# Gates as 1 + tanh instead of sigmoid, in a decoder layer on one Trainium2 core

## The chip, the cores and the metric

The kernel runs on one core of a Trainium2 chip. Its engines run side by side, each through an instruction list of its own, in order: PE multiplies matrices, DVE and ACT do elementwise work, POOL a little more of it, and SP issues the DMA transfers. An engine stops at an instruction until the semaphores that it waits for have been raised by other engines or by a landed transfer. The metric is the device time of one execution in microseconds (us).

## What is computed

One decoder layer on 512 tokens of width 1024, all in float32, then a final norm. Its two attention branches have 8 heads each: one looks back over a window of 128, with sinks, the other attends to blocks of 256. What matters here:

```python
cs = jax.nn.silu(c)
mod = cs @ ada_w[l] + ada_b[l]
shift1, scale1, gate1, shift2, scale2, gate2 = jnp.split(mod, N_MOD, axis=-1)
h = modulate(rmsnorm(x, norm1_g[l]), shift1, scale1)
proj = h @ w_in[l]
qa, ka, va, qb, kb, vb, ga, gb = jnp.split(proj, offsets, axis=-1)
ya = swa_attention(...) @ w_branch_a[l]
yb = moba_attention(...) @ w_branch_b[l]
merged = jax.nn.sigmoid(ga) * ya + jax.nn.sigmoid(gb) * yb
x = x + gate1[:, None, :] * (merged @ w_out[l])
h2 = modulate(rmsnorm(x, norm2_g[l]), shift2, scale2)
y = jnp.square(jax.nn.relu(h2 @ w_mlp_in[l])) @ w_mlp_out[l]
x = x + gate2[:, None, :] * y
```

## The kernel before

Every float32 product is done as three matmuls of halves: `split` (L71, L72) lets ACT copy the upper half of a tile (names ending in h) and DVE subtract it to get the lower half (names ending in l), and `mm3` (L76 to L78) multiplies high by high, high by low and low by high. So each weight tile passes through DMA, ACT and DVE before PE can use it.

The program runs through these stages. Up to about 70 us: the conditioning vector (`cond`, on the tile `cs`), the first norm and modulation, and part of the input projection. From 70 to about 175 us: the eight windowed heads (tiles named with a: `sa`, `pa`, `ta`), with the q, k, v projections of the other branch (`pqk`) beside them. From about 150 us: the eight block-sparse heads (tiles with b: scores `sb`, probabilities `pb`, their transposes `tb`, split as `ptb`, and head outputs `ob`). Each head's softmax is an Exp activation on ACT at L438, one per 128 queries, after a maximum on DVE (L434, L437). Beside these heads, `run` advances a generator of dense work by the numbers in the table PACE. In this stage that work is `gated(0, keep)`: for each 128 of the 1024 output channels n it makes a gate (`pg` = h times a slice of w_in, weights `gw0n`, then the sigmoid into `sg` at L568) and, one step later, a slice of the branch's output projection (`py`, weights `bw0n`), and `keep` (L593) multiplies the two into `term[n]`. A second generator, `mod_second`, advanced beside it, makes the modulation of the second norm (`ac` at L149 and L151, `pm` at L158) from loads named `a`.

From about 263 to 345 us the heads are over and `gated(1, merge)` does the same for the second branch. `merge` (L672) multiplies, adds `term[n]`, splits the sum into `mhi` and `mlo`, and `first` multiplies the former sum with w_out into `wo`, with weights `ow` from the load `wor`. Beside it `mod_row` builds the row of gate1 (tile `ma` from loads `mw`, sums over partitions in `pr`, bias added at L193). After 345 us come the second norm and the MLP: matmuls into `ph` and `mo`, last into `ml`.

PE is bound to the written order in the early stage and near the second norm; elsewhere a scheduler sets the order of all engines when the program is built. Weight loads share three buffers (`raw`), and the DMA into one is issued on SP once the last reader of its former content, mostly a DVE instruction, is through. ACT evaluates functions from a table that holds one set at a time: where an activation needs a function that the set loaded does not hold, the build puts an ACT_TABLE_LOAD ahead of it, which shows in the profile as an instruction of that activation's line.

Of the kernel before, what the change touches and what calls it, by code (L numbers as in the profile page):

```python
# [10 lines left out]
F32 = mybir.dt.float32  # L11
F32R = mybir.dt.float32r
AF = mybir.ActivationFunctionType
ALU = mybir.AluOpType

P = 128
D = 1024
S = 512
KT = D // P
# [18 lines left out]
def decoder_layer(ctx: ExitStack, tc: tile.TileContext, x, c, ada_w, ada_b, norm1_g, norm2_g, w_in,  # L38
# [3 lines left out]
    V, A, G, SY = nc.vector, nc.scalar, nc.gpsimd, nc.sync  # L42

    pz = ctx.enter_context(tc.tile_pool(name="pz", bufs=1, side="right"))
# [5 lines left out]
    def bank(name):  # L50
        return ps.tile([P, 512], F32, tag="bank", name=name)

    def raw(name):
        return p0.tile([P, 2048], F32, tag="raw", name=name, bufs=3)
# [8 lines left out]
    def small(name):  # L63
        return ptile(p0, [P, 512], name, "s", 2)

    def scratch(name, dt=F32):
        return p0.tile([P, 512], dt, name=name, tag="t", bufs=3)

    def split(hi, lo, src):

        A.activation(hi, src, AF.Copy)  # L71
        V.tensor_tensor(lo, src, hi.bitcast(F32), op=ALU.subtract)  # L72

    def mm3(o, w, m, first=True, last=True, **kw):

        nc.tensor.matmul(o, w[0], m[0], start=first, stop=False, **kw)  # L76
        nc.tensor.matmul(o, w[0], m[1], start=False, stop=False, **kw)  # L77
        nc.tensor.matmul(o, w[1], m[0], start=False, stop=last, **kw)  # L78

    def at(pair, *idx):  # L80
        return tuple(t[idx] for t in pair)
# [4 lines left out]
    def chain(*gens):  # L86
        for g_ in gens:
            yield from g_
# [17 lines left out]
    def slot(n, name, dt=F32):  # L106

        return p0.tile([P, 512], dt, name=name, tag=f"slot{n}")
# [14 lines left out]

    cols = pz.tile([P, 64], F32, name="cols")
    cs = pz.tile([P, KT], F32, name="cs")
    bcol = cols[:, 0:48]

    def cond(crow):

        pst = bank("pst")  # L130
        nc.tensor.transpose(pst[:, :KT], crow, ident[:KT, :KT])
        A.activation(cs, pst[:, :KT], AF.Sigmoid)
        V.tensor_mul(cs, cs, pst[:, :KT])

    def rows(stack):
        pst = bank("pst2")
        nc.tensor.transpose(pst[:, :64], stack, ident[:64, :64])
        V.tensor_copy(cols, pst[:, :64])
# [25 lines left out]
        V.tensor_mul(ab[:, 1:2], ab[:, 1:2], cols[:, gain + f:gain + f + 1])  # L164
        V.tensor_add(ab[:, 0:1], pm[:, 0:1], bcol[:, b0:b0 + 1])

    def mod_row(v, dst, pool):

        for half in range(2):
            acc = pool.tile([P, 512], F32, name=f"ma{v}{half}", tag="macc", bufs=1)  # L170
            c0 = v * D + half * 512
            for kk in range(2):
                t = raw(f"mw{v}{half}{kk}").rearrange("p (k n) -> p k n", k=4)
                SY.dma_start(t, ada_w[0].rearrange("(k p) n -> p k n", p=P)[:, 4 * kk:4 * kk + 4, c0:c0 + 512])
                yield
                for k in range(4):
                    c1 = cs[:, 4 * kk + k:4 * kk + k + 1]
                    if kk + k == 0:
                        V.tensor_scalar(acc, t[:, k], c1, None, op0=ALU.mult)
                    else:  # L180
                        V.scalar_tensor_tensor(acc, t[:, k], c1, acc, op0=ALU.mult, op1=ALU.add)  # L181
                    if k % 2:
                        yield
            b = dst[half]
            SY.dma_start(b, ada_b[:, c0:c0 + 512].to_broadcast([P, 512]))
            ah, al = (p0.tile([P, 512], F32R, name=f"ma{v}{half}{i}", tag="t", bufs=3) for i in "hl")
            split(ah, al, acc)
            for _ in range(3):
                yield
            pr = bank(f"pr{v}{half}")  # L190
            nc.tensor.matmul(pr, ones_r, ah, start=True, stop=False)
            nc.tensor.matmul(pr, ones_r, al, start=False, stop=True)
            V.tensor_tensor(b, pr, b, op=ALU.add)  # L193
            yield

    ab2 = pz.tile([P, KT, 2], F32, name="ab2")
# [1 line left out]
    def mod_second():  # L198
        for f in range(KT):
            ad = ada_load(3, f, raw(f"a2{f}"))  # L200
            yield
            acc = pz.tile([P, 2, P], F32, name=f"ac2{f}", tag="acc2", bufs=1)
            yield from mod_cols(f, 3, 56, ad, acc, ab2[:, f])

    with ExitStack() as sa:
# [28 lines left out]
        with ExitStack() as ss:  # L234
# [134 lines left out]
            for f in range(KT):  # L369
                for i, _ in enumerate(project(f, 2 if f == 0 else 0, NT)):  # L370
# [4 lines left out]
                    if i == 2 and f + 2 in starts:  # L375
                        n = starts[f + 2]
# [147 lines left out]
        def cols_of(wr, half, name):  # L524
            w = wide(name)
            split(w[0], w[1], wr[:, :, half * P:(half + 1) * P])
            return w
# [23 lines left out]
        def gated(s, use):  # L551

            wr = br = sg = None
            wb = (w_branch_a, w_branch_b)[s]
            for n in range(KT + 1):
                m, before = n - 1, sg
                if n < KT:
                    if n % 2 == 0:
                        wr = raw(f"gr{s}{n}").rearrange("p (k n) -> p k n", k=KT)
                        SY.dma_start(wr, w0[:, :, (C_GA, C_GB)[s] + n * P:(C_GA, C_GB)[s] + (n + 2) * P])  # L560
                    w = cols_of(wr, n % 2, f"gw{s}{n}")
                    pg = bank(f"pg{s}{n}")
                    for k in range(KT):
                        mm3(pg, at(w, slice(None), k), at(hT, slice(None), k), first=k == 0, last=k == KT - 1)
                        if k == 3:
                            yield
                    sg = scratch(f"sg{s}{n}")
                    A.activation(sg, pg, AF.Sigmoid)  # L568
                    yield
                if m < 0:  # L570
                    continue
                if m % 2 == 0:
                    br = p0.tile([P, 4, 256], F32, name=f"br{s}{m}", tag="br")
                    cc = slice(m * P, (m + 2) * P)
                    if s == 0:
                        for g in range(2):
                            SY.dma_start(br[g * 64:(g + 1) * 64],
                                         wb[0, g * 256:(g + 1) * 256, cc].rearrange("(j d) n -> d j n", d=64))
                    else:
                        SY.dma_start(br, wb[0, :, cc].rearrange("(j p) n -> p j n", p=P))  # L580
                u = tuple(v.rearrange("p (j n) -> p j n", j=4) for v in small(f"bw{s}{m}"))
                split(u[0], u[1], br[:, :, (m % 2) * P:(m % 2 + 1) * P])
                py = bank(f"py{s}{m}")
                for k in range(4):
                    mm3(py, at(u, slice(None), k), at(attnT[s], slice(None), k), first=k == 0, last=k == 3)
                use(m, py, before)
                yield

        term = {}

        def keep(n, py, sg):
            term[n] = slot(n, f"term{n}")
            V.tensor_tensor(term[n], py, sg, op=ALU.mult)  # L593

        def run(heads, dense, per):

# [17 lines left out]
        def beside(gen, other, n):  # L614
            for _ in gen:
                advance(other, n)
                yield

        ms = mod_second()
        second_branch = gated(1, lambda *a: merge(*a))  # L620
        last_head = run([lambda n=n: swa_head(n) for n in range(8)] + [lambda n=n: moba_head(n) for n in range(8)],
            chain(proj_v(0), proj_qk(0), proj_v(1), beside(chain(proj_qk(1), gated(0, keep)), ms, 2),
                  islice(second_branch, 1)), PACE)

# [21 lines left out]
    with ExitStack() as sb:  # L646
        pb = sb.enter_context(tc.tile_pool(name="pb", bufs=1, reuse_waits="tile"))
        g1row = pb.tile([P, D], F32, name="g1row")
# [12 lines left out]
        def out_second(b):  # L661
            wr = raw(f"wo2r{b}").rearrange("p (k n) -> p k n", k=4)
            SY.dma_start(wr, wo[:, 4 * b:4 * b + 4, 512:1024])
            w = (p0.tile([P, 4, 512], F32R, name=f"wo2{b}h", tag=f"at{b}h"),
                 p0.tile([P, 4, 512], F32R, name=f"wo2{b}l", tag=f"at{b}l"))
            wo2.append(w)
            for k in range(4):
                yield
                V.tensor_mul(wr[:, k], wr[:, k], g1row[:, 512:])
                split(w[0][:, k], w[1][:, k], wr[:, k])  # L670

        def merge(n, py, sg):  # L672
            V.tensor_tensor(sg, py, sg, op=ALU.mult)
            V.tensor_add(sg, sg, term[n])
            mlo[n] = slot(n, f"mlo{n}", F32R)
            split(mhi[:, n], mlo[n], sg)
            if n:
                first(n - 1)
# [8 lines left out]
            for t in range(NT):  # L687
                mm3(po[t], merged(n, t), w, first=n == 0, last=n == KT - 1)

        side = chain(ms, mod_row(2, (g1row[:, :512], g1row[:, 512:]), pb), out_second(0))  # L690
        for n, _ in enumerate(second_branch):
            if n == 0:
                last_head.finish()
# [92 lines left out]
    side = mod_row(5, g2row, pc)  # L786
    for h in range(2):
        SY.dma_start(frow[h], final_g.rearrange("(o d) -> o d", o=1)[:, h * 512:(h + 1) * 512].to_broadcast([P, 512]))
    for ci, (f0, f1) in enumerate(CHUNKS):
# [35 lines left out]
        else:  # L825
# [15 lines left out]
            for t in range(NT):  # L841
                o = [slot(4 + 2 * (t % 2) + h, f"o{t}{h}") for h in range(2)]
                cuts = ((0, 512), (512, 1024)) if t < NT - 1 else ((0, 512), (512, 768), (768, 1024))
                sq, n = ssq[:, 4 * (t % 2):4 * (t % 2) + 4], len(cuts) - 1
# [73 lines left out]
```

## Time and profile before

| | |
|---|---|
| time, median of 3 runs | 743.43 us (742.57 to 744.89) |
| the profiled execution | 740.15 us, its span 738.4 us |
| PE busy | 704.9 us, 95% of the span |
| DVE, ACT, POOL busy | 469.4, 353.8 and 28.8 us |
| the chain that ended last | PE 82%, DMA 5%, ACT 4%, DVE 4% |
| DMA | 96.79 MB, 131 GB/s over the span |

The span is the time from the first to the last instruction in the profile. The chain is followed back from the last instruction, at each step to what released it, so an engine's share in it is time that the end depended on. Busy time of an engine that is off the chain costs nothing by itself. Matmuls are pipelined: one of 512 columns is shown as 0.39 us long, though the next one can start earlier.

### The profile page before, as it was taken

What the parts mean: (1) busy time and instruction counts of PE and PEld (TensorE: products, weight loads), DVE (VectorE), ACT (ScalarE), POOL (GpSimd) and SP (SyncE); (2) the same over time, 40 slices, a digit from 0 to 9 for tenths busy, and PEclk for the clock granted to TensorE, in tenths of its full rate; (3) what the DMA queues carried; (4) which work ended last, traced back from release to release, by engine and by line L of the source; (5) the groups of instructions that cost most, each with busy time, mean ns of one, the idle gap of its engine ahead of it and who ended that gap; (6) DMA issues with size and microseconds to landing.
All of it is one profiled execution on the core that took longest, in us unless ns stands there. A gap on an engine that the chain in (4) does not pass through costs nothing.

```text
span 738.4 us, 9237 instructions
## 1 busy us (share of the span) xinstructions
PE 704.9 (95%) x3442; PEld 590.8 (80%) x3442; DVE 469.4 (64%) x973; ACT 353.8 (48%) x649; POOL 28.8 (4%) x40
## 2 busy tenths in 40 slices
PE   3789999898999999999999999999999999999996
PEld 1677989787887888888888888888888888888885
DVE  4876799887877788674487663262643527336765
ACT  3446798776987753432374342231342214322334
POOL 2220000000000000000310000000000000000001
PEclk9999999999999999999999999999999999999999
DMA  8992241554454756461315452224331432224103
GB/s 301 305 286 75 72 129 29 140 161 129 137 150 142 270 172 216 155 200 57 115 58 172 136 193 70 79 92 121 108 115 57 122 103 83 92 68 160 58 0 115
DMA packets 89065, 96.79 MB, mean 131 GB/s; under 512 B 2611, under 2 KB 70267, under 8 KB 89020
## 3 DMA queue, kind: packets, MB, share of 16 engines
q1 hardware_dynamic: 89020, 96.20, 41.9%
q8 instruction: 27, 0.44, 0.2%
q14 instruction: 18, 0.15, 0.1%
HBM read 94.03 MB, written 2.16 MB: 130 GB/s over the span
## 4 chain that ended last, share of the span: by engine, by line
PE 82%; DMA 5%; ACT 4%; DVE 4%; SPq 3%; issue 1%; POOLq 0%; POOL 0%; ACTq 0%; DVEq 0%
PE ph L77 8%; PE ph L78 8%; PE ph L76 8%; PE mo L78 7%; PE mo L77 7%; PE mo L76 7%; PE pg L76 3%; PE pg L77 3%; PE pg L78 3%; SPq L259 2%; DMA ad<-in_ada_w_dram 2%; PE pqk L78 2%; PE pqk L76 2%; PE pqk L77 2%; PE py L76 2%; PE py L78 2%
## 5 line engine op out<-in xcount | busy, mean ns | idle before, releaser
L794 ACT ACTIVATE r<-ph 128x512 f32<-128x512 f32 x32 | 18.8, 586 | 41.7 <-PE ph L78 26.8
L797 DVE TENSOR_TENSOR r<-r 128x512 f32<-128x512 f32 x32 | 21.9, 689 | 18.2 <-ACT a1h L796 8.0
L151 DVE SCALAR_TENSOR_TENSOR ac<-a,cs,ac 128x256 f32<-128x256 f32 x56 | 26.6, 476 | 2.7 <-ACT ac L149 2.3
L287 DVE SCALAR_TENSOR_TENSOR pac<-ad,cs,pac 128x256 f32<-128x256 f32 (+1 forms) x42 | 21.4, 522 | 10.4 <-ACT pac L285 10.0
L705 DVE TENSOR_TENSOR rs<-mo,g2row 128x512 f32<-128x512 f32 x24 | 15.9, 686 | 9.3 <-PE mo L78 9.3
L121 POOL TENSOR_TENSOR rstd<-rstd,mhalf 128x1 f32<-128x1 f32 x12 | 7.3, 615 | 372.7 <-DVE rstd L120 372.7
L181 DVE SCALAR_TENSOR_TENSOR ma<-mw,cs,ma 128x512 f32<-128x512 f32 x28 | 21.0, 749 | 0.5
L76 PE MATMUL g0p<-hTh,g0h 128*128 128x512 f32 (+1 forms) x36 | 16.1, 448 | 3.8 <-ACT hTh L71 3.8
L438 ACT ACTIVATE pb<-pb,nb 128x128 f32<-128x128 f32 (+3 forms) x32 | 17.8, 557 | 2.0 <-DVE nb L437 1.8
L706 DVE TENSOR_TENSOR x_sb<-x_sb,rs 128x512 f32<-128x512 f32 x24 | 16.1, 683 | 0.0
L438 ACT ACTIVATE pa<-pa,na 128x256 f32<-128x256 f32 (+1 forms) x32 | 15.2, 476 | 0.8 <-DVE na L437 0.6
L434 DVE CUSTOM_DVE_ANT_0 pb<-sb,tm 128x128 f32<-128x128 f32 (+3 forms) x32 | 15.2, 483 | 0.1
L77 PE MATMUL g0p<-hTl,g0h 128*128 128x512 f32 (+1 forms) x36 | 14.7, 409 | 0.0
L78 PE MATMUL g0p<-hTh,g0l 128*128 128x512 f32 (+1 forms) x36 | 14.4, 399 | 0.0
L434 DVE CUSTOM_DVE_ANT_0 pa<-sa,ts,sink 128x256 f32<-128x256 f32 (+1 forms) x32 | 13.4, 445 | 1.2 <-PE sa L433 1.1
L433 PE MATMUL sb<-qk,qk 128*128 128x128 f32 (+3 forms) x64 | 12.7, 330 | 0.0
L76 PEld LDWEIGHTS g0p<-hTh,g0h 128*128 128x128 f32 x36 | 8.0, 222 | 5.2 <-ACT hTh L71 4.5
L292 PEld LDWEIGHTS pac<-ones_r,acc 128*128 128x128 f32 x32 | 5.6, 242 | 7.9 <-DVE acc L287 4.4
L72 DVE TENSOR_TENSOR qk<-pqk,qk 64x512 fp32r<-64x512 f32 x16 | 11.0, 688 | 1.3 <-ACT qk L71 0.8
L292 PE MATMUL pac<-ones_r,acc 128*128 128x1 f32 x32 | 5.4, 276 | 6.7 <-DVE acc L287 6.7
L275 POOL TENSOR_TENSOR g0l<-g0r,g0h 128x512 fp32r<-128x512 f32 x8 | 10.6, 1321 | 29.4 <-ACT g0h L274 29.4
L706 POOL TENSOR_TENSOR x_sb<-x_sb,rs 128x512 f32<-128x512 f32 x4 | 5.1, 1302 | 156.4 <-DVE rs L705 156.4
(1590 smaller groups left out, 2423.7 us busy)
## 6 DMA issues: line engine op xcount, KB each, us to landing
mi<-in_w_mlp_in_dram SPq DMA_DIRECT2D x16, 1024.0 KB, 5.8
mo<-in_w_mlp_out_dram SPq DMA_DIRECT2D x14, 1024.0 KB, 5.0
ad<-in_ada_w_dram SPq DMA_DIRECT2D x16, 512.0 KB, 7.7
a<-in_ada_w_dram SPq DMA_DIRECT2D x16, 512.0 KB, 5.0
gr<-in_w_in_dram SPq DMA_DIRECT2D x8, 1024.0 KB, 6.4
mw<-in_ada_w_dram SPq DMA_DIRECT2D x8, 1024.0 KB, 5.3
x_sb<-in_x_dram SPq DMA_DIRECT2D x8, 512.0 KB, 6.5
qkr<-in_w_in_dram SPq DMA_DIRECT2D x4, 1024.0 KB, 5.5
```

The lines of the kernel that those rows point to most:

```text
L76: nc.tensor.matmul(o, w[0], m[0], start=first, stop=False, **kw)
L77: nc.tensor.matmul(o, w[0], m[1], start=False, stop=False, **kw)
L78: nc.tensor.matmul(o, w[1], m[0], start=False, stop=last, **kw)
L151: V.scalar_tensor_tensor(acc, ad[:, k], cs[:, k:k + 1], acc, op0=ALU.mult, op1=ALU.add)
L181: V.scalar_tensor_tensor(acc, t[:, k], c1, acc, op0=ALU.mult, op1=ALU.add)
L287: V.scalar_tensor_tensor(part_ if k < KT - 1 else acc, ad(k), cs[:, k:k + 1], part_, op0=ALU.mult, op1=ALU.add)
L434: V.tensor_tensor_reduce(p[:, o:o + w], pb[:, :w], b[:, w - 1::-1] if w < b.shape[1] else b[:, ::-1], scale=SCALE, scalar=-3e38 if sk is N ...
L438: A.activation(p[:, o:o + w], p[:, o:o + w], AF.Exp, bias=neg[:, i:i + 1], accum_out=sums[:, i:i + 1])
L705: V.tensor_tensor(tm, p_, row[half], op=ALU.mult)
L706: add.tensor_tensor(x_sb[:, t, cc], x_sb[:, t, cc], tm, op=ALU.add)
L794: A.activation(r, ph, AF.Relu)
L797: V.tensor_mul(r, r, r)
```

## The change

The sigmoid is written as (1 + tanh(x/2)) / 2. ACT evaluates Tanh with a scale of 0.5 in place of Sigmoid, in `cond` and in `gated`. The sum with one is taken inside the product with the branch: DVE's instruction `scalar_tensor_tensor` does (sg + 1) * py in place of the plain product, in `keep` and in `merge`. The half is taken out of both terms and put into the row of gate1, which multiplies the merged branches later: `mod_row` is called with `csh`, half of `cs`, and adds half the bias. In `cond`, two small DVE instructions on 128 x 8 are added.

```diff
     cs = pz.tile([P, KT], F32, name="cs")
+    csh = pz.tile([P, KT], F32, name="csh")
...
-        A.activation(cs, pst[:, :KT], AF.Sigmoid)
+        A.activation(cs, pst[:, :KT], AF.Tanh, scale=0.5)
+        V.tensor_scalar(cs, cs, 0.5, 0.5, op0=ALU.mult, op1=ALU.add)
         V.tensor_mul(cs, cs, pst[:, :KT])
+        V.tensor_scalar(csh, cs, 0.5, None, op0=ALU.mult)
...
-    def mod_row(v, dst, pool):
+    def mod_row(v, dst, pool, scale=1.0, cs=cs):
...
-            V.tensor_tensor(b, pr, b, op=ALU.add)
+            V.scalar_tensor_tensor(b, b, scale, pr, op0=ALU.mult, op1=ALU.add)
...
-                    A.activation(sg, pg, AF.Sigmoid)
+                    A.activation(sg, pg, AF.Tanh, scale=0.5)
...
-            V.tensor_tensor(term[n], py, sg, op=ALU.mult)
+            V.scalar_tensor_tensor(term[n], sg, 1.0, py, op0=ALU.add, op1=ALU.mult)
...
-            V.tensor_tensor(sg, py, sg, op=ALU.mult)
+            V.scalar_tensor_tensor(sg, sg, 1.0, py, op0=ALU.add, op1=ALU.mult)
...
-        side = chain(ms, mod_row(2, (g1row[:, :512], g1row[:, 512:]), pb), out_second(0))
+        side = chain(ms, mod_row(2, (g1row[:, :512], g1row[:, 512:]), pb, 0.5, csh), out_second(0))
```

In the built program, PE, POOL and SP have the same instructions in the same order before and after, with the same waits. Three places show what moved on the other two.

ACT's rows before, around the fourth gate of the first branch, where the softmax of the fifth block-sparse head runs beside it (this is 207 to 217 us of the profile):

```order
L71 ACTIVATE at1h<-ob_2187 64x512
L438 ACT_TABLE_LOAD
L438 ACTIVATE pb_2229,ub_2231<-pb_2229,nb_2232 128x128
L71 ACTIVATE gw05h<-gr_2332 128x1024
L438 ACTIVATE pb_2229,ub_2231<-pb_2229,nb_2232 128x256
L568 ACT_TABLE_LOAD
L568 ACTIVATE sg_2277<-pg_2202 128x512
L227 ACTIVATE qk_1712<-pqk_1830 64x512
L71 ACTIVATE ptb30h<-tb_2283 128x512
L71 ACTIVATE ptb31h<-tb_2292 128x512
L71 ACTIVATE ptb32h<-tb_2301 128x256
L438 ACT_TABLE_LOAD
```

The same rows of the changed kernel:

```order
L71 ACTIVATE at1h<-ob_2190 64x512
L441 ACTIVATE pb_2232,ub_2234<-pb_2232,nb_2235 128x128
L71 ACTIVATE gw05h<-gr_2335 128x1024
L441 ACTIVATE pb_2232,ub_2234<-pb_2232,nb_2235 128x256
L571 ACTIVATE sg_2280<-pg_2205 128x512
L230 ACTIVATE qk_1715<-pqk_1833 64x512
L71 ACTIVATE ptb30h<-tb_2286 128x512
L71 ACTIVATE ptb31h<-tb_2295 128x512
L71 ACTIVATE ptb32h<-tb_2304 128x256
L441 ACTIVATE pb_2232,ub_2234<-pb_2232,nb_2235 128x384
```

The three loads are gone and nothing else has moved. Over the whole program 17 loads become one, the one at the first activation.

DVE's rows before at the first product of `merge` (282 us), with the sums for gate1's row, `ma`, around it:

```order
L72 TENSOR_TENSOR gw13l<-gr_3019,gw13h 128x1024
L181 SCALAR_TENSOR_TENSOR ma_2944<-mw_2968,cs,ma_2944 128x512
L673 TENSOR_TENSOR sg_2933<-py_2995,sg_2933 128x512
L181 SCALAR_TENSOR_TENSOR ma_2944<-mw_2968,cs,ma_2944 128x512
L674 TENSOR_TENSOR sg_2933<-sg_2933,term_2052 128x512
```

The same rows of the changed kernel:

```order
L72 TENSOR_TENSOR gw13l<-gr_3022,gw13h 128x1024
L184 SCALAR_TENSOR_TENSOR ma_2947<-mw_2971,csh,ma_2947 128x512
L676 SCALAR_TENSOR_TENSOR sg_2936<-sg_2936,py_2998 128x512
L184 SCALAR_TENSOR_TENSOR ma_2947<-mw_2971,csh,ma_2947 128x512
L677 TENSOR_TENSOR sg_2936<-sg_2936,term_2055 128x512
```

The product is another kind of instruction in the same place, and `ma` reads `csh`.

DVE's rows before at the start, where `cond` makes `cs` (3 us):

```order
L243 MEMSET rbx 33x16
L97 TENSOR_SCALAR ones_r<-ident 128x128
L133 TENSOR_TENSOR cs<-cs,pst 128x8
L287 SCALAR_TENSOR_TENSOR pac_154<-ad_109,cs,pac_154 128x512 x2
L350 COPY rv_165<-prv_164 16x512
```

The same rows of the changed kernel:

```order
L246 MEMSET rbx 33x16
L97 TENSOR_SCALAR ones_r<-ident 128x128
L134 TENSOR_SCALAR cs<-cs 128x8
L135 TENSOR_TENSOR cs<-cs,pst 128x8
L136 TENSOR_SCALAR csh<-cs 128x8
L290 SCALAR_TENSOR_TENSOR pac_157<-ad_110,cs,pac_157 128x512 x2
L353 COPY rv_168<-prv_167 16x512
```

Two instructions of 8 columns are added ahead of the first modulation sum, `pac`.

## Rows read from the trace of the kernel before

**Rows 1.** The page: busy time of PE, and the granted clock of TensorE in 40 equal slices of the span, in tenths.

```profile
PE 704.9 (95%) x3442; PEld 590.8 (80%) x3442; DVE 469.4 (64%) x973; ACT 353.8 (48%) x649; POOL 28.8 (4%) x40
...
PEclk9999999999999999999999999999999999999999
```

**Rows 2.** Busy time by stretch: stretch and its length in us, then busy us (and instructions) of PE, PEld, DVE, ACT and POOL, the granted clock, the share of the DMA engines and GB/s.

```profile
70.00:120.00 50.00, 50.00 (x326) 45.47 (x325) 44.08 (x137) 41.93 (x102) 1.04 (x2) 1.00 0.27 77
...
176.00:263.00 87.00, 82.82 (x425) 69.14 (x424) 68.93 (x191) 73.00 (x129) 1.16 (x3) 1.00 0.50 152
263.00:345.00 82.00, 82.00 (x372) 68.18 (x371) 58.16 (x89) 31.70 (x49) 0.00 (x0) 1.00 0.51 167
```

**Rows 3.** The table loads of the lines L438 and L568: number, length in ns (least, median, most), and the first and the last start in us. The last row is one of them in ACT's timeline, the second of L438's: start us, length us.

```profile
L438 ACT ACT_TABLE_LOAD  x8: 1283/1283/1283, 79.0 to 254.8; - x8
...
L568 ACT ACT_TABLE_LOAD  x8: 1283/1283/1283, 177.7 to 260.9; - x8
...
182.07 1.28 ACT L438 ACT_TABLE_LOAD   x1
```

**Rows 4.** PE's timeline at four places of the stretch from 176 to 263 us, and at one place for comparison (205 us): start us, length us, instruction, and in brackets the idle time before it and who ended it.

```profile
179.63 0.50 PE L76 MATMUL pg<-hTh,gw01h 128*128 128x512 f32 x1 [2.83 <-ACT sg L568]
...
205.07 1.52 PE L433 MATMUL sb<-qk,qk 128*128 128x128 f32 x8
206.43 0.40 PE L78 MATMUL pg<-hTh,gw03l 128*128 128x512 f32 x1
...
219.08 0.40 PE L78 MATMUL pg<-hTh,gw04l 128*128 128x512 f32 x1
220.23 0.61 PE L158 MATMUL pm<-ones_r,ac 128*128 128x1 f32 x4 [0.75 <-DVE ac L151]
...
230.69 0.39 PE L76 MATMUL pg<-hTh,gw05h 128*128 128x512 f32 x1
230.92 0.39 PE L77 MATMUL pg<-hTl,gw05h 128*128 128x512 f32 x1
231.80 0.50 PE L474 MATMUL ob<-ptb40h,vb 128*128 128x512 f32 x1 [0.50 <-ACT ptb40h L71]
...
236.55 1.53 PE L433 MATMUL sb<-qk,qk 128*128 128x128 f32 x8
238.18 0.50 PE L76 MATMUL pg<-hTh,gw06h 128*128 128x512 f32 x1
```

**Rows 5.** ACT's timeline ahead of the first of these places, with the same columns.

```profile
176.62 1.06 ACT L71 ACTIVATE gw02h<-gr 128x1024 fp32r<-128x1024 f32 x1 [2.12 <-PE tb L463]
177.69 1.28 ACT L568 ACT_TABLE_LOAD   x1
178.98 0.60 ACT L568 ACTIVATE sg<-pg 128x512 f32<-128x512 f32 x1
```

**Rows 6.** The chain that ended last, in order of time: start us, length us, engine, tile and line of each piece. A piece "ACT L438" or "ACT L568" without a tile is a table load.

```profile
205.21 1.40 PE sb L433 x8
...
207.86 1.28 ACT L438
...
211.11 1.28 ACT L568
...
215.03 1.28 ACT L438
...
219.78 0.40 DVE ac L151
...
220.20 6.42 DMA gr<-in_w_in_dram
...
226.64 1.07 ACT gw06h L71
...
231.15 0.61 ACT ptb40h L71
...
236.26 1.26 ACT L568
```

**Rows 7.** ACT's timeline behind that transfer, with the columns of rows 4, and the time from issue to landing of the transfers into `gr` from 215 to 300 us.

```profile
227.72 1.28 ACT L438 ACT_TABLE_LOAD   x1
...
DMA to landing us min/median/max: 5.4/6.2/8.6
```

**Rows 8.** Groups of instructions on DVE, with line, operation, number | busy us, mean ns of one | idle time of DVE before them, and who ended it.

```profile
L181 DVE SCALAR_TENSOR_TENSOR ma<-mw,cs,ma 128x512 f32<-128x512 f32 x28 | 21.0, 749 | 0.5
L673 DVE TENSOR_TENSOR sg<-py,sg 128x512 f32<-128x512 f32 x8 | 5.5, 689 | 5.9 <-PE py L78 5.9
L593 DVE TENSOR_TENSOR term<-py,sg 128x512 f32<-128x512 f32 x8 | 5.5, 684 | 0.9 <-PE py L78 0.9
L287 DVE SCALAR_TENSOR_TENSOR pac<-ad,cs,pac 128x512 f32<-128x512 f32 x6 | 4.5, 744 | 6.0 <-ACT pac L285 6.0
```

**Rows 9.** ACT's timeline behind the stretch, at the first weights of w_out, and the matmul of PE that uses them, with the columns of rows 4.

```profile
287.79 0.63 ACT L71 ACTIVATE ow0h<-wor 128x512 fp32r<-128x512 f32 x1 [2.23 <-DMA wor<-in_w_out_dram]
...
289.50 1.07 PE L76 MATMUL wo<-ow0h,mhi 128*128 128x512 f32 x4
```

**Rows 10.** The start of the program: DVE makes `cs`, and ACT uses it first.

```profile
2.99 0.16 DVE L133 TENSOR_TENSOR cs<-cs,pst 128x8 f32<-128x8 f32 x1 [0.31 <-ACT cs L132]
...
8.43 0.69 ACT L285 ACTIVATE pac<-ad,cs 128x512 f32<-128x512 f32 x1 [5.47 <-DMA ad<-in_ada_w_dram]
```

## The prediction

> **What bounds the kernel now.** [...] Then I asked where the instructions that go away stand. One of the 17 table loads is the first activation's and stays. Eight are L438's and eight L568's, 1283 ns each [rows 3]: 16 x 1.283 = 20.5 us of ACT. The first of L438's is at 79.0 us, where PE is busy 50.00 of 50.00 us [rows 2, 3], so it is worth nothing; L438's second comes at 182.07. So 15 lie between 177 and 262 us, which is why the view by stretches is cut at 176 and 263: there ACT is busy 73.00 of 87 us, 19.2 us of it table loads, and PE 82.82, so PE idles 4.18 us in all. Behind it, to 345 us, PE does not idle at all [rows 2]. That is the first number to hold on to: of 19.2 us that ACT gets back in this stretch, no more than about 4 can reach the end.
>
> PE's timeline gives the places: four stops, of 2.83, 0.75 and 0.50 us and a small one at 238 us [rows 4]. For each I asked who was late, in ACT's timeline [rows 5, 7] and in the chain of work that ended last [rows 6]. The chain is telling: from 205.21 to 238 us it leaves PE and runs through ACT, DVE and a transfer, with four loads as pieces of their own. PE's matmuls of 512 columns follow at 0.23 us (230.69 to 230.92), so a start's delay is its distance from the matmul before, less 0.23; that is a little more than the idle time shown, because the shown length of a matmul runs past the next one's start.
>
> **What the change takes out, stop by stop.**
>
> Stop 1, 179.63 us. PE waits for the first gate, `sg`. ACT had to do the weights `gw02h` first, which it could start only at 176.62, when PE let it; then the load from 177.69 to 178.97; then the gate [rows 5]. Without the load the gate begins at 177.69 at the latest: 1.28 us. The other 1.55 us of this stop stay, since ACT began on PE's word and `gw02h` and the gate take 1.06 and 0.60.
>
> [...]
>
> Stop 2, 220.23 us. PE waits for DVE's `ac`, 220.23 - 219.08 - 0.23 = 0.92 us late. The chain to it starts at PE's `sb` at 205.21, and passes loads at 207.86, 211.11 and 215.03 before `ac` at 219.78 [rows 6]. Its start moves up 1.28 with PE, its length shrinks by 3 x 1.28 = 3.84: `ac` is through at 220.18 - 5.12 = 215.06, and PE asks for it at 219.31 - 1.28 = 218.03. The stop goes, with 2.97 us to spare.
>
> Stop 3, 231.80 us. PE waits for `ptb40h`, 231.80 - 230.92 - 0.23 = 0.65 us late. Here ACT stood still for the load of `gr`, issued at 220.20, the moment `ac` had left its buffer, and landed 6.42 us later [rows 6]. With `ac` early the issue moves to about 215.1 and the landing to 221.5. From `gw06h` to the end of `ptb40h` is 231.76 - 226.64 = 5.12 us, with a load in it at 227.72 [rows 7], so 3.84 without. `ptb40h` is ready at about 225.4; PE asks at 231.15 - 1.28 - 0.92 = 228.95. It goes too, with 3.5 us to spare, 2.3 if that load was hidden behind DVE's half of the weights.
>
> Stop 4, 238.18 us. The same eight small matmuls take 1.36 us to the next one at 205.07 and 1.63 here, so PE is 0.27 us late [rows 4]. The gate it waits for has a load directly ahead, at 236.26 [rows 6]: 1.28 against 0.27.
>
> Sum: 1.28 + 0.92 + 0.65 + 0.27 = 3.12 us. After 238 us three loads of ACT's go that PE did not wait for; they are ease, not gain.
>
> **What it adds.** The products become instructions of another kind. The rows nearest to it are 749 ns (both sources in SBUF) and 744 ns (the accumulator in PSUM) for 128 x 512, against 684 and 689 for the products of today [rows 8]. I take 60 ns more, with bounds of 0 and 65: 20 instructions (16 products, four rows of L193), 1.2 us of DVE. DVE is busy 68.93 of 87 and 58.16 of 82 us [rows 2], and the first product that PE's next short need hangs on is the one ahead of `ow0h`, which is ready at 288.42 for a matmul at 289.50 [rows 9]: 1.08 us in hand. So it costs nothing; without that cover, 0.06 us a product.
>
> [...]
>
> In `cond` two DVE instructions on 8 columns are added, 0.16 us each by the one that is there [rows 10]. `cs` is then ready at about 3.5 us; ACT first uses it at 8.43, having waited 5.47 us for a transfer. Hidden, unless that transfer came 4.9 us earlier. Tanh for Sigmoid: 0.60 us for 128 x 512 [rows 5], the length of ACT's plain copy `ptb40h` of that size, 0.60 to 0.61 [rows 6]; I take no difference.
>
> So 740.15, the profiled execution's own time, becomes 737.0. The runs shown have their median at 743.43, 0.4% above that execution; I take the same 3.1 us off: 740.3.
>
> **The rivals.**
>
> Capped (0.20). PE is 3.1 us ahead and meets something that has not moved. Two places could do it. If `gr` still landed at 226.62, `ptb40h` would be ready at 231.76 - 1.28 = 230.48 and PE, asking at 228.95, would be held 1.53 us: 1.6 us of gain are left, 741.8. For it: ACT did stand for that transfer. Against: its issue follows `ac` by 0.02 us. Or `ow0h`, 1.08 us in hand, could stay where it is, held by its own transfer, for which ACT waited 2.23 us [rows 9]: 1.1 us are left, 742.3. Against: that transfer too waits for DVE's work behind ACT's loads.
>
> [...]
>
> Nothing (0.08). The time won is lost again at a wait in the MLP or at the end, or the table is loaded as often as before: 743.4. The order of the built program shows one load, so the second way is all but out.
>
> Slower (0.06). `gr`, issued five us earlier, could share the DMA engines with the loads issued before it and land late. From its issue at 215.1, with 3.84 us behind it, PE is back at today's time when it lands at about 227.9, after 12.8 us, and above that loses one for one; slower by 0.3% at 15 us, 745.7. The longest transfer of this kind took 8.6 [rows 7].
>
> **How the numbers follow.** The forecast, all four stops, has 0.60: 740.3, with its own range from 739.6 to 741.1 for the idle times against the delays and a stop that shrinks but stays. The range reaches from the longer switch (738.9, less 0.2 for small delays that no row shows) to the capped cases (742.3, and 0.2): 738.7 to 742.5. It leaves out nothing and slower, 0.14. A difference below 0.3%, 2.2 us, can't be told from none here. Faster takes the forecast and the longer switch, 0.66, less 0.04 for a forecast that measures short: 0.62. Same takes the capped cases, nothing and that 0.04: 0.32. Slower: 0.06.
>
> **What the changed kernel's profile would show.** One table load, and ACT's busy time down by about 20.5 us, to 333. The stop at the second gate's first matmul shortened from 2.83 to about 1.55, and no stop at `pm`, `ptb40h` and `pg` of `gw06h`. PE idle in this stretch down from 4.18 to about 1.6 us, and PE still without a gap to 345. If the stops go and the span doesn't follow, it is lost behind 263 us, and PE's idle time there shows where. [...] What would make me wrong: a new stop of PE for a transfer, or a stop 1 that another wait fills.

## The result and the profile after

The changed kernel takes 739.5 us (median of 30 executions, 735.6 to 744.0), the kernel before 743.8 (77 executions, 740.7 to 748.4). The two were timed side by side twice: the first time (22 executions of each) gives a ratio of 0.9942, with a 95% interval of 0.9925 to 0.9959, the second 0.9930 (0.9904 to 0.9956). That is 4.3 us less, where 3.1 were forecast, and 739.5 us where 740.3 were.

The page of the changed kernel, its busy times and TensorE's granted clock, against [rows 1], and the two stretches against [rows 2] (busy us of PE, PEld, DVE, ACT and POOL, the clock, DMA). This execution took 744.04 us:

```profile
PE 709.9 (96%) x3442; PEld 595.7 (80%) x3442; DVE 470.2 (63%) x975; ACT 333.3 (45%) x633; POOL 28.8 (4%) x40
...
PEclk9999999989999999999999999999999999999998
...
176.00:263.00 87.00, 84.69 (x435) 72.12 (x434) 71.97 (x206) 55.73 (x120) 1.56 (x3) 0.98 0.55 165
263.00:345.00 82.00, 82.00 (x375) 68.30 (x374) 57.39 (x88) 30.31 (x47) 0.00 (x0) 1.00 0.51 167
```

ACT is busy 333.3 us (353.8 before), 17.3 us less in the first of the two stretches; DVE's busy time hardly changes (470.2 us against 469.4), and PE's idle time from 176 to 263 us falls from 4.18 to 2.31 us. The same stretch in a second profile of the same kernel, which took 739.83 us, has 1.44 us:

```profile
176.00:263.00 87.00, 85.56 (x444) 72.96 (x443) 74.78 (x208) 55.98 (x120) 1.56 (x3) 1.00 0.56 167
```

Two things in the first profile call for an explanation: it is an execution of the faster kernel that is slower than the one profiled before (744.04 against 740.15 us), and PE is busy 5 us longer in it. The granted clock gives both. Four stretches of this profile, cut where its clock changes:

```profile
140.00:147.27 7.27, 5.45 (x31) 4.47 (x29) 7.14 (x18) 6.03 (x15) 0.52 (x1) 1.00 0.40 97
147.27:154.10 6.83, 6.07 (x18) 5.03 (x19) 6.64 (x22) 5.36 (x15) 0.00 (x0) 0.50 0.95 278
154.10:184.82 30.72, 28.41 (x150) 24.19 (x150) 21.60 (x61) 16.44 (x33) 1.04 (x2) 1.00 0.46 135
184.82:188.23 3.41, 3.41 (x10) 2.64 (x9) 3.28 (x7) 3.39 (x9) 0.00 (x0) 0.50 0.00 0
```

Twice here, and once more at 58.53 us, TensorE's granted clock was 0.50 and not 1.00, for 3.41 or 6.83 us. PE's timeline shows what that costs (start us, length us, instruction, and in brackets the idle time and who ended it):

```profile
148.03 1.59 PE L466 MATMUL ta<-ident,pa 128*128 128x128 f32 x6 [2.58 <-DVE pa L452]
...
183.92 0.50 PE L76 MATMUL pg<-hTh,gw01h 128*128 128x512 f32 x1 [2.31 <-ACT sg L571]
184.26 0.40 PE L77 MATMUL pg<-hTl,gw01h 128*128 128x512 f32 x1
184.49 0.39 PE L78 MATMUL pg<-hTh,gw01l 128*128 128x512 f32 x1
...
185.91 0.63 PE L76 MATMUL pg<-hTh,gw01h 128*128 128x512 f32 x1
186.34 0.63 PE L77 MATMUL pg<-hTl,gw01h 128*128 128x512 f32 x1
```

Matmuls of 512 columns that follow at 0.23 us elsewhere follow at 0.43 us there, so a stretch of 3.41 us sets PE back by 1.6 us, as an estimate from these two steps: 3.41 x (1 - 0.23 / 0.43). Each of the two comes close to a stop of PE: the first begins within one of 2.58 us for `ta`, which the change does not touch, the second 0.9 us after stop 1. The profile on which the prediction rests had none of these stretches ahead of the last few us: it was an execution with a mean granted clock of 0.998, while the kernel before has 0.993 on average. By the slope below that is 2.9 of the 3.3 us between it and the median.

The mean granted clock is on record for 172 executions (not for the 22 of the kernel before in the first comparison), so the kernels can be compared at one clock. A straight line through all of them, with one slope and a level for each kernel, has a slope of 0.60 us for each 0.001 of clock (about 0.06 either way) and leaves a scatter of 1.0 us. The experiments ran in three batches, each on a chip of its own with the kernel before beside it, and at equal clock the kernel before lay 1.2 us (0.7) higher in the second batch than in the third. The last column therefore gives each batch a level of its own too (there the kernel after rests on the eight executions of the first batch):

| kernel | executions | median, us | mean clock | level against before at equal clock, us (95%) | the same, within its batch |
|---|---|---|---|---|---|
| before | 77 | 743.8 | 0.9932 | 0 | 0 |
| after | 30 | 739.5 | 0.9942 | -3.9 (0.4) | -3.8 (0.8) |
| only the first gate by tanh | 12 | 740.8 | 0.9958 | -1.5 (0.7) | -1.5 (0.7) |
| all gates but the first | 12 | 740.9 | 0.9922 | -3.2 (0.6) | -3.2 (0.6) |
| before, products in the new form | 12 | 743.5 | 0.9937 | +0.1 (0.6) | -0.3 (0.7) |
| after, two loads put back | 12 | 744.0 | 0.9926 | -0.2 (0.6) | -0.6 (0.7) |
| after, first gate ahead of gw02h | 6 | 737.0 | 0.9963 | -5.5 (0.9) | -5.9 (0.9) |
| the same, and ta earlier | 5 | 735.5 | 0.9980 | -5.4 (1.0) | -5.8 (1.0) |
| the same, gw02h behind the softmax | 6 | 735.3 | 0.9962 | -7.3 (0.9) | -6.5 (1.0) |

So the change is worth 3.9 us at equal clock. The other 0.6 us go with the mean clock, which is 0.0009 higher; but that difference has an interval of 0.0011 either way, so it is not shown that the change itself makes the clock fall less often.

### The profile page after: what moved, and what is told of

Read it like the earlier page. It is cut to its first block, busy times and chain, and to the rows that moved or that the text cites. A ratio compares the mean times of both kernels' runs of the same rounds, so it can differ in the third digit from the quotient of the medians.

```text
span 742.2 us, 9223 instructions
## 1 busy us (share of the span) xinstructions
PE 709.9 (96%) x3442; PEld 595.7 (80%) x3442; DVE 470.2 (63%) x975; ACT 333.3 (45%) x633; POOL 28.8 (4%) x40
## 4 chain that ended last, share of the span: by engine, by line
PE 83%; DMA 5%; DVE 4%; SPq 3%; ACT 2%; issue 1%; POOLq 0%; POOL 0%; ACTq 0%; DVEq 0%
PE ph L78 8%; PE ph L77 8%; PE ph L76 8%; PE mo L78 6%; PE mo L77 6%; PE mo L76 6%; PE pg L76 4%; PE pg L77 4%; PE pg L78 4%; SPq L262 2%; DMA ad<-in_ada_w_dram 2%; PE py L78 2%; PE py L76 2%; PE py L77 2%; PE pqk L76 2%; PE pqk L77 2%
## 5 line engine op out<-in xcount | busy, mean ns | idle before, releaser
L466 PE MATMUL ta<-ident,pa 128*128 128x128 f32 x56 | 8.8, 294 | 2.6 <-DVE pa L452 2.6
```

## The experiments

Three theories were put to the test. One: the four stops are the whole gain. Two: a stop also leaves a stretch at a granted clock of 0.50 behind it, and part of the gain is that. Three: something outside the stops is won.

**Both kernels again.** Nothing is edited.

> The kernel before, unchanged, for the granted clock of its executions beside those of the kernel after. Theory one (the four stops of TensorE in 176 to 263 us, 3.12 us by the prediction, are the whole of the change, and the rest of the measured 4.3 us is scatter): at an equal mean clock its executions lie about 3.1 us above those of the kernel after, and the mean clocks of the two are alike. Theory two (each stop also leaves a stretch at the half clock behind it, which the change takes away with the stop): its mean clock is lower than that of the kernel after by some 0.001 to 0.002, at about 0.8 us for each 0.001, and the gap at an equal clock stays 3.1 us or less. Theory three (something beside the stops is won): the gap is 4 us or more at an equal clock.

> The kernel after, unchanged. All theories: about 4 us under the kernel before. [...] By theory three PE's gaps outside 176 to 263 us are shorter than in the kernel before too.

Measured: 743.34 us (its comparison with executions of the same kernel gave 0.9978, 0.9957 to 0.9999, which shows what such a comparison can be off by) and 739.45. In the second profile of the kernel before stop 1 was 3.4 us long, and 6.83 us at a granted clock of 0.50 went with it:

```profile
182.47:189.30 6.83, 5.58 (x13) 4.43 (x14) 4.55 (x10) 6.72 (x13) 0.00 (x0) 0.50 0.04 12
```

None of the three theories fits as it stood. The level of 3.9 us is above the 3.1 of one and two, and the clock differs the way two says, but by no more than its scatter. Three holds in part: 0.8 us are won outside the four stops, as the next comparison shows, and they lie in the same stretch from 176 to 263 us.

The rest can be laid side by side matmul by matmul, since PE runs the same 3442 matmuls in the same order in both kernels and in the next three. From the 200th to the 650th (63 to 131 us in the trace of before) all of them take 68.06 us, within 0.02. So the load at 79 us was worth nothing, as forecast. From the 1050th to the 1300th (212 to 263 us), where stops 2 to 4 lie, the kernel before takes 50.86 and 50.88 us, the kernel after 48.24 in both profiles: 2.63 us, where 0.92 + 0.65 + 0.27 = 1.84 were counted. PE's timeline of the kernel after (second profile) at these three places, against [rows 4]:

```profile
220.96 0.39 PE L78 MATMUL pg<-hTh,gw04l 128*128 128x512 f32 x1
221.19 0.50 PE L161 MATMUL pm<-ones_r,ac 128*128 128x1 f32 x4
...
231.78 0.39 PE L77 MATMUL pg<-hTl,gw05h 128*128 128x512 f32 x1
232.00 0.39 PE L477 MATMUL ob<-ptb40h,vb 128*128 128x512 f32 x1
232.23 0.39 PE L78 MATMUL pg<-hTh,gw05l 128*128 128x512 f32 x1
...
237.97 0.40 PE L76 MATMUL pg<-hTh,gw06h 128*128 128x512 f32 x1
```

No idle time is shown at any of them, and the matmuls of 512 columns start 0.22 to 0.24 us behind the one ahead: the stops gave 0.92, 0.66 and 0.26 us, as counted. But the matmul behind gains too. In the kernel before it stood 0.34 us behind the one that had waited:

```profile
231.80 0.50 PE L474 MATMUL ob<-ptb40h,vb 128*128 128x512 f32 x1 [0.50 <-ACT ptb40h L71]
232.14 0.39 PE L78 MATMUL pg<-hTh,gw05l 128*128 128x512 f32 x1
```

That is 0.11 us for each of the three. A fifth place had no bracket at all, since the idle time is hidden in the shown length of the scores `sb` (0.97 us in both, with the next `ob` 0.93 us behind their start before and 0.81 after); before, and after (second profile):

```profile
245.10 0.97 PE L433 MATMUL sb<-qk,qk 128*128 128x128 f32 x6
246.03 0.49 PE L474 MATMUL ob<-ptb50l,vb 128*128 128x512 f32 x1
...
247.43 0.40 PE L76 MATMUL py<-at0h,bw05h 128*128 128x512 f32 x1
```

```profile
244.80 0.97 PE L436 MATMUL sb<-qk,qk 128*128 128x128 f32 x6
245.61 0.39 PE L477 MATMUL ob<-ptb50l,vb 128*128 128x512 f32 x1
...
246.76 0.39 PE L76 MATMUL py<-at0h,bw05h 128*128 128x512 f32 x1
```

From `sb` to `py` 2.33 us became 1.96. So 0.33 + 0.37 of the missing 0.79 us lie at small waits in the same stretch, and 0.1 in steps too small to name. The two kernels that keep the loads there but differ otherwise, the next one and the one with the new products, take 50.70 us, so 2.5 of the 2.6 us go with the loads.

**One gate alone, and all gates but that one.** A gate that keeps the sigmoid gets the factor 2 in its product. The edit is shown in part, for the first gate alone, where `cond` keeps the sigmoid too; the other kernel has the opposite condition.

```diff
+    def tanh(s, n):
+        return s == 0 and n == 0
+
+    def product(s, n, dst, py, sg):
+        c, op = (1.0, ALU.add) if tanh(s, n) else (2.0, ALU.mult)
+        V.scalar_tensor_tensor(dst, sg, c, py, op0=op, op1=ALU.mult)
```

> Only the first gate of the first branch by tanh, so that the two table loads at stop 1 (177.69 and 182.07 us in the trace of the kernel before) go and fifteen stay; the other gates keep the sigmoid, with the factor 2 in their product, and the result is the same. Theory one: 1.28 us under the kernel before (742.6 where that has 743.8), the other three stops as they were, moved earlier by that. Theory two: the same, and more where a stretch at half clock behind stop 1 goes with it; up to 3 us. Theory three: the stop stays where a DMA of the gate's branch is late (gr02h landed so in the profile of the kernel after), so 0.5 us or nothing.

> All gates by tanh but the first of the first branch, so that only the two table loads at stop 1 stay beside the first load. Theory one: stops 2, 3 and 4 go, 0.92 + 0.65 + 0.27 = 1.84 us under the kernel before, and stop 1 is as it was (2.83 us). Theory two: stop 1 still leaves its half-clock stretch, so 1.84 us or less. Theory three: more than 2.5 us, with the gain outside the four stops.

Measured: 740.8 us (0.9954, 0.9934 to 0.9974) and 740.9 (0.9965, 0.9942 to 0.9987). The waits of PE in the two (engine, tile and line, what it waited for: us, times, longest), first the one gate, then the others:

```profile
PE pg L76 <- ACT sg L577: 1.7, 1, 1.7
...
PE pm L167 <- DVE ac L160: 0.7, 1, 0.7
...
PE ob L483 <- ACT ptb40h L71: 0.4, 1, 0.4
```

```profile
PE pg L76 <- ACT sg L578: 3.2, 1, 3.2
```

The two halves come apart at the places forecast: with the first gate changed only stop 1 shrinks and the others stay, and with the others changed only stop 1 is left. The parts add up within the scatter (1.5 and 3.2 against 3.9). The size of the second was missed: 1.84 us were expected and the level fell by 3.2 (0.6), of which PE's steps from the 1050th to the 1300th matmul show the 2.63 us of the kernel after. The first gate alone took 3.1 us off the median and 1.5 off the level: the rest is its clock, 0.9958 against 0.9932. That is on the side of theory two, but the kernel after, with fewer stops still, has 0.9942. ACT's timeline at stop 1 corrects the prediction, first with the load kept, then without:

```profile
179.05 1.06 ACT L71 ACTIVATE gw02h<-gr 128x1024 fp32r<-128x1024 f32 x1 [2.51 <-DMA gr<-in_w_in_dram]
180.13 1.28 ACT L578 ACT_TABLE_LOAD   x1
181.42 0.60 ACT L578 ACTIVATE sg<-pg 128x512 f32<-128x512 f32 x1
```

```profile
177.31 1.06 ACT L71 ACTIVATE gw02h<-gr 128x1024 fp32r<-128x1024 f32 x1 [2.41 <-DMA gr<-in_w_in_dram]
178.27 0.58 ACT L577 ACTIVATE sg<-pg 128x512 f32<-128x512 f32 x1
```

ACT stood at `gw02h` for its transfer and not for PE. In the trace of before the view had named PE there [rows 5], but the transfer had been issued at 169.48 and landed 7.1 us later, at 176.5, 0.1 us before `gw02h` began:

```profile
169.48 0.37 SPq L560 DMA_DIRECT2D gr<-in_w_in_dram  x1
...
DMA to landing us min/median/max: 7.1/7.1/7.1
```

In ten of the eleven profiles `gw02h` begins 0.02 to 0.1 us after its transfer has landed; in the eleventh, of the experiment that puts it further back, it comes later.

**Two loads put back.** Two activations on one column ahead of the first gate, by two functions, each with a load of its own (the part of the edit that adds them).

```diff
+                    last = None
+                    for j, f in enumerate((AF.Sigmoid, AF.Exp) if (s, n) == (0, 0) else ()):
+                        with tc.issue_after(last.ins) if last else ExitStack():
+                            last = A.activation(pz.tile([P, 1], F32, name=f"one{j}"), pg[:, :1], f)
```

> The kernel after with two table loads put back directly ahead of the first gate, between the weights gw02h and the gate, and nothing else moved: two activations on one column, one by the sigmoid and one by Exp, each with a load of 1.283 us in front. Theory one (a stop costs its own length): stop 1 grows by two loads and two small instructions of about 0.2 to 0.3 us, 3.0 us, so 739.5 becomes 742.5, at the mean clock of the kernel after (0.994). [...]

Measured: 744.0 us, all of the gain gone. ACT's timeline and PE's wait:

```profile
178.15 1.06 ACT L71 ACTIVATE gw02h<-gr 128x1024 fp32r<-128x1024 f32 x1 [2.03 <-DMA gr<-in_w_in_dram]
179.22 1.28 ACT L574 ACT_TABLE_LOAD   x1
180.52 0.17 ACT L574 ACTIVATE one<-pg 128x1 f32<-128x1 f32 x1
180.69 1.28 ACT L574 ACT_TABLE_LOAD   x1
181.99 0.17 ACT L574 ACTIVATE one<-pg 128x1 f32<-128x1 f32 x1
182.06 0.59 ACT L576 ACTIVATE sg<-pg 128x512 f32<-128x512 f32 x1
...
PE pg L76 <- ACT sg L576: 4.3, 1, 4.3
```

Two loads and two small instructions take 2.84 us, from 179.22 to 182.06, and PE's stop is 4.30 us instead of 1.44 (2.31 in the other profile of the kernel after). So the price of a switch in this kernel is 1.28 us, with 0.02 us to the next instruction. The median rose by 4.5 us, where the longer stop gives 2.9. Within the batches the level rose by 3.2 us (1.0), 0.3 of it outside the span, so the level is the stop's length as far as can be told; the clock fell to 0.9926, by 0.0016 with an interval as wide, about 1.0 us. Its profile has 6.83 us at a granted clock of 0.50 from 181.45 us on.

**The first gate first.** ACT issues the first gate ahead of `gw02h`.

```diff
-                    w = cols_of(wr, n % 2, f"gw{s}{n}")
+                    with tc.issue_after(gates[0].ins) if (s, n) == (0, 2) else ExitStack():
+                        w = cols_of(wr, n % 2, f"gw{s}{n}")
...
-                    A.activation(sg, pg, AF.Tanh, scale=0.5)
+                    gates.append(A.activation(sg, pg, AF.Tanh, scale=0.5))
```

> The kernel after with ScalarE's first gate issued ahead of the weights gw02h, whose transfer it stands for, instead of behind them. If what stays of stop 1 is that transfer (issued 172.75, ScalarE held until 179.91 in the second profile of the kernel after) and not TensorE's word, as the prediction had it, the stop goes whole: 1.4 us off, 738.1; by theory two 0.5 to 1 us more, with a mean clock above 0.994. If TensorE holds ScalarE there, the gate comes no earlier and nothing changes: 739.5.

Measured: 737.0 us, 0.9900 (0.9875 to 0.9925), and 1.6 us (0.9) under the kernel after at equal clock. ACT's and PE's timelines:

```profile
176.60 0.60 ACT L573 ACTIVATE sg<-pg 128x512 f32<-128x512 f32 x1 [0.44 <-PE pg L78]
178.47 1.06 ACT L71 ACTIVATE gw02h<-gr 128x1024 fp32r<-128x1024 f32 x1 [1.28 <-DMA gr<-in_w_in_dram]
```

```profile
178.22 0.48 PE L76 MATMUL pg<-hTh,gw01h 128*128 128x512 f32 x1
```

The gate starts as soon as PE's last product for it is through, `gw02h` still waits for its transfer, now behind it, and PE does not stop. (In this kernel and the next two the scheduler also puts 92 to 122 of PE's 3442 matmuls in other places, in this one all of them behind stop 1.) So what stayed of stop 1 was that transfer ahead of the gate in ACT's queue, and all of it could be won.

**The stop at 145 us too.** DVE divides the last windowed head's probabilities ahead of the weights `qkw30l`.

```diff
-                    w = cols_of(wr[s], half, f"qkw{i}{s}")
+                    with tc.issue_after(norm["a7"].ins) if (i, s) == (3, 0) else ExitStack():
+                        w = cols_of(wr[s], half, f"qkw{i}{s}")
```

> The same, and VectorE divides the last windowed head's probabilities by their sums ahead of the lower half of the weights qkw30 instead of behind it, which shortens the stop of 2.5 us at 145 us (TensorE's transposes ta wait for them). Theory one: 1.2 to 1.5 us less than with the first gate moved alone, 736.7. Theory two: the half-clock stretch that all profiles but the first show behind this stop goes or becomes rarer, 1.7 us more and a mean clock of 0.996 or above: 735. Rival: the weights qkw30, later by 0.8 us, make a stop of their own at their first use, and 0.8 us of the gain are lost.

Measured: 735.5 us, 0.9888 (0.9863 to 0.9914). The stop shrank as forecast, and a new one came, as the rival had it, though at another place than named. The waits of PE, then ACT and PE around the new stop:

```profile
PE ta L468 <- DVE pa L454: 1.4, 1, 1.4
PE py L76 <- ACT qk L230: 1.3, 1, 1.3
```

```profile
176.02 1.06 ACT L71 ACTIVATE gw02h<-gr 128x1024 fp32r<-128x1024 f32 x1 [2.82 <-DMA gr<-in_w_in_dram]
...
180.87 0.59 ACT L230 ACTIVATE qk<-pqk 64x512 fp32r<-64x512 f32 x1
```

```profile
181.51 0.50 PE L76 MATMUL py<-at0h,bw00h 128*128 128x512 f32 x1 [1.34 <-ACT qk L230]
```

The stop at 145 us shrank by 1.1 us, and PE, earlier by that, ran into the queue behind `gw02h`. The level did not move (-5.4 against -5.5). What moved is the clock, 0.9980 against 0.9963 (five and six executions, 0.0016 either way), and this profile has no stretch at 0.50 ahead of the last few us.

**The waiting weights further back.** `gw02h` goes behind the next head's softmax (`eb2`, its last Exp) instead of behind the first gate.

> As the kernel with both moves, but the weights gw02h, which stand for a transfer, go behind the next head's softmax on ScalarE and no longer ahead of it. In the profile with both moves ScalarE stood 2.82 us at gw02h (until 176.02) with that softmax and the head's copies queued behind, and TensorE's py at 181.51 stood 1.34 us for the last of them. If the queue behind the waiting instruction is the cause, that stop goes and nothing takes its place: 1.3 to 1.6 us less, 734.0, profile with no stop above 0.8 us after the one at 145 us. Rival: gw02h, later by some 4 us, makes a stop of its own at the first matmul with it, and the time stays at 735.5.

Measured: 735.3 us, 0.9880 (0.9853 to 0.9908). The new stop is gone. The two stretches that held the stop at 145 us and stop 1:

```profile
140.00:160.00 20.00, 18.60 (x100) 15.66 (x99) 18.03 (x52) 14.95 (x34) 0.52 (x1) 1.00 0.62 178
170.00:190.00 20.00, 20.00 (x107) 17.10 (x107) 16.29 (x46) 13.77 (x28) 1.04 (x2) 1.00 0.65 190
```

PE is busy 20.00 of 20 us where the kernel before had stop 1, and what is left of the stop at 145 us is 1.4 us. From the 650th to the 1300th matmul, the same ones in the kernel with both moves and in this one, PE takes 127.04 us there and 125.64 here, and the granted clock of neither profile falls to 0.50 in between: 1.4 us less, as expected, with nothing in its place. The median is only 0.2 us lower, and not the 734.0 forecast. The executions do not show more: the first of the table's level columns puts this kernel 1.9 us under the one with both moves, but the two ran in different batches, and within the batches it is 0.8 us (1.4 either way). The six executions had a mean clock of 0.9962, and that of the one profiled fell to 0.50 at 58.19 us, ahead of all that was edited. That it is the faster of the two is therefore shown by one profile of each alone. Against the kernels before and after it is faster by either measure.

**The new products without the rest.** The kernel before, with its products and rows in the two-operation form.

```diff
-            V.tensor_tensor(term[n], py, sg, op=ALU.mult)
+            V.scalar_tensor_tensor(term[n], sg, 0.0, py, op0=ALU.add, op1=ALU.mult)
...
```

> The kernel before with its sixteen products and the four rows of gate1 and gate2 written as the two-operation instruction (the sum with zero, or the product with one, put in), sigmoid and all seventeen table loads kept. By the rows of the kernel after (681 to 687 ns for the new form, 684 to 689 for the old) the same time as the kernel before, 743.8, within 0.3. If the new form itself helps or costs something that the profile hides, that difference shows here.

Measured: 743.5 us, 0.9996 (0.9975 to 1.0016). The form of the product alone changes nothing that shows (0.3 us, 0.7 either way, within the batch).

## Why the prediction was right, point by point

**PE's idle time is the limit: right.** Of ACT's 20.5 us, 3.9 reach the end, and they come out of PE's waits from 176 to 263 us, those hidden in shown lengths included.

**Stop 1: right size, wrong cause.** From the last transpose `tb` to `pg` PE took 3.11 to 3.64 us in the four profiles with one load ahead of the gate (3.41 on average), and 1.71 to 2.58 in the three with none (2.09). The difference is 1.3 us, the load, and it would be that with either cause, since the load stands between `gw02h` and the gate. But the step "since ACT began on PE's word" failed: it was the transfer into `gr`, and the 1.55 us said to stay are no floor. They were 1.44, 1.70 and 2.31 us in three profiles, and the profile with the gate moved ahead has none of them.

**Stops 2 to 4: right, with some luck.** 0.92, 0.66 and 0.26 us, against 0.92, 0.65 and 0.27. In the kernel after `ac` was ready 2.0 us before PE asked, where 2.97 were reckoned: against PE the chain to it shrank by 2.8 us, and not by three whole loads. So the transfer of `gr` was issued a microsecond later than reckoned, but it landed after 5.5 us instead of 6.42, and the 3.5 us to spare at `ptb40h` came out as forecast with an error on either side. ACT still stood 1.7 us for that transfer, but it was no cap. At stop 4 the gate was ready 1.3 us ahead.

**"They are ease, not gain": this term was too small, by 0.8 us.** The step set aside the loads after 238 us (four in ACT's timeline, from 239.54 us on, and not three), and the sum left out what a stop costs the matmul behind it. The traces showed 0.11 us behind each of three stops and 0.37 at 246 us. With all of it the sum is 1.3 + 2.63 = 3.9 us, which is what was measured at equal clock.

**"The same 3.1 us off" the median: incomplete.** The base was one execution at a clock of 0.998, and its row of nines [rows 1] is not the kernel's. The gap of 3.3 us to the median was left without a cause. By the slope 2.9 us of it go with the clock. So do 0.6 us of the measured 4.3, but that part is within the scatter of the clock.

**The products: right that they cost nothing, wrong in the 60 ns.** DVE in the kernel after, against [rows 8]:

```profile
L676 DVE SCALAR_TENSOR_TENSOR sg<-sg,py 128x512 f32<-128x512 f32 x8 | 5.5, 686 | 6.6 <-PE py L78 6.5
...
L596 DVE SCALAR_TENSOR_TENSOR term<-sg,py 128x512 f32<-128x512 f32 x8 | 5.4, 681 | 1.8 <-PE py L78 1.6
```

681 to 686 ns, where the plain form took 684 to 689: the lower bound of 0 was the right one. The 749 ns of L181 belong to an instruction whose factor `cs` is a column in SBUF; here it is a constant. Whether that is the cause was not tried.

**The rivals.** The low end of the range starts from 738.9 and a longer switch, 0.06 of the chances; no run shows that term, and each of the two loads put back took 1.28 us, with the next instruction 0.02 us behind it. "Nothing" is out by the times, and the table is loaded once. "Slower" needed a transfer of 12.8 us, and it took 5.5. Capped did not come: PE is busy 82.00 of 82 us from 263 to 345, so `ow0h` held nothing up; in the MLP PE waits for weights `miw` now and then, but from its 1300th matmul to the end it takes 468.4 and 468.6 us in the kernel after and 468.0 to 469.2 in the four profiles of kernels with fifteen or seventeen loads, so no gain is given back there that rises above this scatter.

**What stays open.** Why the clock falls in one execution and not in the next. At or right behind the stop of 2.5 us at 145 us it fell in eight of nine profiles, at the same stop of 1.4 us in none of two. Around stop 1 it fell at 2.31, 3.37 and 4.30 us, and did not at 2.83, 3.1 and 3.2, nor at 1.44, 1.70 or without a stop. The mean clocks lean to theory two (0.9931 over the 113 executions with the whole stop 1 or more, 0.9946 over 42 with the shortened one, 0.9968 over 17 without it; intervals of 0.0005 to 0.0007). But the groups are not of one piece: the middle one holds 0.9942 (the kernel after) and 0.9958 (the first gate alone, which keeps stops 2 to 4), the last one holds two kernels in which the stop at 145 us is shorter too, and no length of a stop tells the two outcomes apart. The stretch at 0.50 between 44 and 62 us, in six of eleven profiles, was left alone.

## What to carry to other kernels

Price the time that is taken off an engine beside the bottleneck by the bottleneck's stops alone. Then count the step behind each stop too: over the whole stretch, compare the distance between starts with that of undisturbed neighbours, since short waits hide in shown lengths (0.37 us at 246 us here). Where the view names a releaser, hold its end against the start that it released, and look for a transfer that landed just then: an instruction that waits for a transfer holds what is queued behind it (ACT stood 2.82 us at `gw02h`, and PE 1.34 us for the last copy in the queue behind it). Moving it back took away two stops of 1.4 and 1.3 us here, beside the 3.9 us of the change itself. Ask why the profiled execution and the median differ before taking one as the base of the other, and compare kernels with a kernel timed beside them, since levels moved by 1.2 us from batch to batch.

## What the runs showed of the chip

Executions of one kernel lay 8 us apart with nothing changed. Most of that goes with TensorE's granted clock (means of 0.988 to 0.998 in the kernel after): ahead of the last few us the profiles show stretches of 3.41 or 6.83 us at a granted clock of 0.50, eleven of seventeen close to the stop at 145 us or to stop 1, and 0.001 of mean clock went with 0.60 us. A matmul of 512 columns started 0.43 us behind the last at that clock and 0.23 at 1.00, and 0.34 behind one that had waited. A table load cost ACT 1.28 us, and the next instruction began 0.01 to 0.02 us behind it.
